# Where the 64x64 triangular inverses of a chunked recurrence are made: GpSimd with 32x32 blocks, or GpSimd with 16x16 blocks and TensorE

## The chip, the cores and the metric

The kernel runs on one core of one Trainium2 chip. The metric is device time in microseconds, the median of the runs; lower is better.

## What is computed

The program is three transformer layers in a row on a sequence of 512 positions with 1024 channels, all in float32 (large matmuls as three products of split float32r halves). The change touches the mixer of the third layer, an RWKV-7 recurrence over 16 heads of 64 channels, once forward and once backward in time:

```
def rwkv7_scan(r, w, k, v, kk, a):
    def step(state, inp):
        r_t, w_t, k_t, v_t, kk_t, a_t = inp
        sa = jnp.einsum('bhvk,bhk->bhv', state, -kk_t)
        state = (state * w_t[:, :, None, :] + sa[..., None] * (kk_t * a_t)[:, :, None, :]
                 + v_t[..., None] * k_t[:, :, None, :])
        return state, jnp.einsum('bhvk,bhk->bhv', state, r_t)
...
    for d in range(2):
        w_log = -jax.nn.softplus(-(w0[d] + jnp.tanh(xw @ w1[d]) @ w2[d])) - 0.5
        decay = jnp.exp(-jnp.exp(w_log.astype(F32)))
        a = jax.nn.sigmoid(a0[d] + (xa @ a1[d]) @ a2[d])
...
        o = rwkv7_scan(*ins)
...
        dir_out.append((group_norm(o, gn_w, gn_b) + bonus.reshape(nB, S, D)) * g.astype(F32))
    y = dir_out[0] + dir_out[1]
    return y.astype(h.dtype) @ w_o
```

The kernel does not step through 512 positions. It cuts them into 8 chunks of 64 and, in each chunk and head, solves with a unit triangular 64x64 matrix I + L. The inverse of that matrix is what the change is about.

## The kernel before

The recurrence is the function `rwkv`. Two heads fill the 128 partitions (head h on partitions 64h to 64h+63), so there are 8 head pairs; with two directions that makes 16 rounds, `q = 0..15`, `p, d = divmod(q, 2)`. A round has four stages, each a Python generator whose `yield`s cut it into steps:

- `pair` (once per two rounds) loads k and r of a head pair and its small weights, and makes normalised keys.
- `prep` makes decays and scaled operands (`ar`, `bk`), multiplies them into `sc` (L1310 on TensorE, masked out of PSUM by VectorE in L1313), and makes the other operands `vs`, `tb`, `za`, `kb`. `sc` holds the triangular matrices; its diagonal 32x32 blocks go to DRAM as `lu` (L1320, queue SP). There are 2 heads x 2 blocks x 8 chunks = 32 such blocks.
- `invert` reads them back as `lt` (L1371), one block per partition and four copies of the 32 blocks, each copy for a quarter of the columns. GpSimd then does 31 elimination steps of two instructions: a product `tmp` (L1378) and a subtraction from `x` (L1380). The result goes to DRAM as `xu` (L1387) and back into the 64x64 layout as `X` (L1391). VectorE transposes the first block (L1399), TensorE multiplies twice (L1406, L1415) and VectorE writes the off-diagonal block (L1419). That completes the inverse.
- `scan` uses `X` (L1434) and then runs the chain over the chunks: six pairs of a TensorE product (L1468) and a VectorE update of `n` (L1469), output products (L1463, L1473) and group norm, gate and accumulation (L1478 to L1504).

Two fillers of lower priority run beside them: `values` (v projection, L1204) and `output` (output projection, L1217, added up by VectorE in L1219). Both load weights through queue SP (L1199, L1211).

A loop over a step counter `t` starts `prep`, `invert` and `scan` of a round at steps 0, 9 and 36 of that round, a round begins every 16 steps, and every step advances each live generator by one `yield`. This gives the order in which instructions are written; a scheduler then orders each engine by priority and by when a buffer slot of a pool is free, and every engine and DMA queue executes its list strictly in order. Pool `bk` has two slots; pool `un` (`lt`, `x`, `tmp`) has one; PSUM pool `psm` has four; `wr`, for the fillers' weights, has three.

Below, a round's "period" is the distance from one round's transposition L1399 to the next one's.

Of the kernel before, what the change touches and what calls it, by code (L numbers as in the profile page):

```python
# [8 lines left out]
F32 = mybir.dt.float32  # L9
F32R = mybir.dt.float32r  # L10
AF = mybir.ActivationFunctionType
# [5 lines left out]
HP, HPA, HPB, HPS, HPO, HP1, HP1B = 300, 50, 50, -300, 0, 300, 300  # L17
S = 512
D = 1024
NT = D // 128  # L20
# [989 lines left out]
class L3:  # L1010
# [117 lines left out]
    def rwkv(self, lp, rkd, vm, tw, ta, sg):  # L1128
        nc, tc, I = self.nc, self.tc, self.I
        with ExitStack() as cx:  # L1130
            pool = lambda n, b, **kw: cx.enter_context(tc.tile_pool(name=n, bufs=b, **kw))
            arp, vsp, bkp, unp, sp, wk = (pool(n, b) for n, b in (
                ("ar", 4), ("vs", 3), ("bk", 2), ("un", 1), ("s3", 2), ("wk", 2)))
            scp = pool("psc", 1, space=PSUM)
            fil = pool("psf", 2, space=PSUM)
            pop = pool("pso3", 1, space=PSUM)
# [1 line left out]
            nc.sync.dma_start(K3, I["const3"])  # L1138
            mask, cmask, cmat, bones = K3[:, 0:128], K3[:, 128:640], K3[:, 640:768], K3[:, 768:770]
            bfull = K3[:, 770:898]  # L1140
            xeye = lp.tile([128, 8, 32], F32, name="xeye")
            nc.sync.dma_start(xeye, I["xeye"])
            gneps = lp.tile([128, 1], F32, name="gneps")
            nc.vector.memset(gneps, 64e-5)
# [4 lines left out]
            a = VEC_AT["k_a"]  # L1149
# [29 lines left out]
            def T():  # L1179
                turn[0] += 1  # L1180
                p, tag = ((sp, "t3"), (self.tmp, "t"), (self.tmp, "t"))[turn[0] % 3]
                return p.tile([128, S], F32, tag=tag, name=tag)
# [82 lines left out]
            def prep(q, C):  # L1265

                p, d = divmod(q, 2)
# [22 lines left out]
                ar = C["ar"] = arp.tile([128, 2, S], F32, tag="ar", name="ar", bufs=3)  # L1290
                ar0, ar1 = ar[:, 0], ar[:, 1]

                bk = bkp.tile([128, 8, 2, 64], F32, tag="bk", name="bk")
# [10 lines left out]
                sc = C["sc"] = [w4(h).rearrange("p (c t) -> p c t", c=8) for h in range(2)]  # L1304
                for g in range(2):
# [7 lines left out]
                        nc.vector.tensor_tensor(sc[h][:, 4 * g:4 * g + 4, :], ps[h].rearrange("p c a t -> p c (a t)"),  # L1313
                                                mask.unsqueeze(1).to_broadcast([128, 4, 128]), op=ALU.mult)
                    yield
                lu = C["lu"] = self.dram.tile([32, 32, 32], F32, tag="lu", name="lu", bufs=2)
                for h in range(2):
                    for b in range(2):
                        p0, u0 = 64 * h + 32 * b, (h * 2 + b) * 8
                        nc.sync.dma_start(lu[u0:u0 + 8].rearrange("c s t -> s c t"),  # L1320
                                          sc[h][p0:p0 + 32, :, 32 * b:32 * b + 32])

                nc.vector.tensor_tensor(kd, flip(r[p], d), kd, op=ALU.mult)
                if d:
# [4 lines left out]
                vs = C["vs"] = vsp.tile([128, 8, 2, 64], F32, tag="vs", name="vs")  # L1329
# [36 lines left out]
            def invert(q, C):  # L1366


                lt = unp.tile([128, 32, 32], F32, tag="lt", name="lt")
                for f in range(4):  # L1370
                    nc.sync.dma_start(lt[32 * f:32 * f + 32], C["lu"])  # L1371
                x = unp.tile([128, 8, 32], F32, tag="x", name="x")
                nc.gpsimd.tensor_copy(x, xeye)
                yield
                for i in range(31):
                    m, n = i // 4 + 1, 31 - i
                    t = unp.tile([128, 80], F32, tag="tmp", name="tmp")[:, :m * n].rearrange("p (m n) -> p m n", m=m)
                    nc.gpsimd.tensor_tensor(t, x[:, :m, i:i + 1].to_broadcast([128, m, n]),  # L1378
                                            lt[:, i:i + 1, i + 1:].to_broadcast([128, m, n]), op=ALU.mult)
                    nc.gpsimd.tensor_tensor(x[:, :m, i + 1:], x[:, :m, i + 1:], t, op=ALU.subtract)  # L1380
                    if i % 2 == 2 - 1:
                        yield
                X = C["x"] = self.hp.tile([128, 8, 64], F32, tag="h", name="X")
                nc.gpsimd.memset(X, 0.0)
                xu = self.dram.tile([32, 8, 4, 32], F32, tag="xu", name="xu", bufs=2)
                for f in range(4):
                    nc.sync.dma_start(xu[:, :, f, :], x[32 * f:32 * f + 32])  # L1387
                for h in range(2):
                    for b in range(2):
                        p0, u0 = 64 * h + 32 * b, (h * 2 + b) * 8  # L1390
                        nc.sync.dma_start(X[p0:p0 + 32, :, 32 * b:32 * b + 32],  # L1391
                                          xu[u0:u0 + 8].rearrange("c m f t -> (m f) c t"))
                yield
                for _ in range(5):
                    yield

                sc = C["sc"]
                t1 = T()[:, :256].rearrange("p (c t) -> p c t", c=8)
                nc.vector.transpose(t1, X[:, :, 0:32])  # L1399
                yield  # L1400
                qt = T()[:, :256].rearrange("p (c t) -> p c t", c=8)
                pq = self.psm.tile([128, 2, 8, 32], F32, tag="mm", name="mm")
                for c in range(8):
                    for h in range(2):
                        a = 64 * h
                        nc.tensor.matmul(pq[a + 32:a + 64, 0, c, :], sc[h][a:a + 32, c, 32:64], t1[a:a + 32, c, :],  # L1406
                                         start=True, stop=True, tile_position=(a, a + 32))
                for h in range(2):
                    a = 64 * h
                    nc.scalar.activation(qt[a + 32:a + 64], pq[a + 32:a + 64, 0], AF.Copy, scale=-1.0)  # L1410
                yield
                for c in range(8):
                    for h in range(2):
                        a = 64 * h
                        nc.tensor.matmul(pq[a:a + 32, 1, c, :], qt[a + 32:a + 64, c, :], X[a + 32:a + 64, c, 32:64],  # L1415
                                         start=True, stop=True, tile_position=(a + 32, a))
                for h in range(2):
                    a = 64 * h
                    nc.vector.tensor_copy(X[a:a + 32, :, 32:64], pq[a:a + 32, 1])  # L1419
                yield  # L1420

            def scan(q, C):
# [78 lines left out]
                else:  # L1501
# [6 lines left out]
            Cs = [{} for _ in range(NQ)]  # L1508
            stages = [lambda q: prep(q, Cs[q]), lambda q: invert(q, Cs[q]), lambda q: scan(q, Cs[q]), lambda q: pair(q // 2)]
            fills = sorted([(2 * 16 * (p - 1) + 2, self.ahead(values(p), HPS)) for p in range(1, NT)] +  # L1510
                           [(2 * 16 * p + 78, self.ahead(output(p), HPS)) for p in range(NT)], key=lambda x: x[0])
            for _ in values(0):
                pass
            live, lf = [], []
            t = -4
            while t <= 36 + (NQ - 1) * 16 or live or lf or fills:
                for st, at in ((2, 36), (1, 9), (0, 0), (3, -4)):
                    q, e = divmod(t - at, 16)
                    if e == 0 and 0 <= q < NQ and not (st == 3 and q % 2):
                        live.append((st, q, stages[st](q)))  # L1520
                live.sort(key=lambda x: (-x[0] % 4, x[1]))
                live = [x for x in live if next(x[2], 0) != 0]
                while fills and fills[0][0] <= t:
                    lf.append(fills.pop(0)[1])
                if t % 3 == 0:
                    lf = [x for x in lf if next(x, 0) != 0]
                t += 1
# [112 lines left out]
def constants():  # L1640

    import numpy as np
    f = np.float32
    i, t = np.arange(128), np.arange(64)
    a = {"upper": (i[:, None] <= i[None]).astype(f)}
    a["causal"] = np.concatenate([np.zeros((128, 384), f), np.where(i[None] <= i[:, None], 0, -1e30).astype(f)], 1)
    n = np.arange(32)
    cm = np.zeros((128, 4, 33), f)
    for b in range(4):
        ok = (16 * n[None] + 31 <= (b * 128 + i)[:, None]) & (n[None] < 31)  # L1650
        cm[:, b, :32] = np.where(ok, 0, -1e30)
        cm[:, b, 32] = ok.any(1)
    a["cmp_mask"] = cm

    d = np.arange(1024) - 512
    n = np.abs(d)
    large = np.minimum(8 + (np.log(np.maximum(n, 1).astype(f) / f(8)) / f(math.log(128)) * f(8)).astype(np.int32), 15)
    bucket = np.where(d > 0, 16, 0) + np.where(n < 8, n, large)
    a["onehot"] = (bucket[None] == np.arange(32)[:, None]).astype(f)
    c = (n <= 64) * 1 + ((n % 4 == 0) & (n <= 256)) * 1 + (n % 16 == 0) * 1  # L1660
    lnc = np.zeros((16, 1024), f)
    lnc[:8] = np.where(c > 0, np.log(np.maximum(c, 1)), -1e30)
    lnc[8:] = np.where(n <= 128, 0, -1e30)
    a["lnc"] = lnc

    s = i % 64
    mask = np.concatenate([s[:, None] < t[None], s[:, None] <= t[None]], 1)
    starts = np.broadcast_to(np.arange(S) % 64 != 0, (128, S))
    same = i[:, None] // 64 == i[None] // 64
    a["const3"] = np.concatenate([mask, starts, np.eye(128) - same / 64, i[:, None] // 64 == np.arange(2)[None], same], 1).astype(f)  # L1670
    x = np.zeros((4, 32, 8, 32), f)
    for h in range(4):
        for m in range(8):
            x[h, :, m, 4 * m + h] = 1
    a["xeye"] = x.reshape(128, 8, 32)
    return a


# [14 lines left out]
```

## Time and profile before

| quantity | value |
|---|---|
| median of 3 runs | 3077.1 us (3075.54 to 3078.77) |
| time of the profiled execution | 3076.38 us |
| its span, first to last instruction | 3074.6 us |
| share of the span busy: PE, DVE, ACT, POOL | 93%, 54%, 44%, 13% |
| L1378 and L1380 on POOL, busy | 165.0 and 168.5 us, 496 instructions each |
| mean granted TensorE clock | 0.959 |

The engines are named as the profile does: PE is TensorE, DVE VectorE, ACT ScalarE, POOL GpSimd, SP the queue that issues most DMAs. The recurrence occupies the span from about 2000 to 2670 us; outside it POOL is nearly idle. A float32 matmul leaves two records in the trace for one instruction of the program.

### The profile page before, as it was taken

What the parts mean: (1) busy time and instruction counts of PE and PEld (TensorE: products, weight loads), DVE (VectorE), ACT (ScalarE), POOL (GpSimd) and SP (SyncE); (2) the same over time, 40 slices, a digit from 0 to 9 for tenths busy, and PEclk for the clock granted to TensorE, in tenths of its full rate; (3) what the DMA queues carried; (4) which work ended last, traced back from release to release, by engine and by line L of the source; (5) the groups of instructions that cost most, each with busy time, mean ns of one, the idle gap of its engine ahead of it and who ended that gap; (6) DMA issues with size and microseconds to landing.
All of it is one profiled execution on the core that took longest, in us unless ns stands there. A gap on an engine that the chain in (4) does not pass through costs nothing.

```text
span 3074.6 us, 49553 instructions
## 1 busy us (share of the span) xinstructions
PE 2859.1 (93%) x19720; PEld 2302.1 (75%) x19720; DVE 1671.7 (54%) x3427; ACT 1356.4 (44%) x2460; POOL 386.7 (13%) x1116
## 2 busy tenths in 40 slices
PE   7999999999999999899999999977788888599998
PEld 6877778778898889776988888856555556388887
DVE  5566684554462335766733446945555656553445
ACT  5565652663342223555532333744454443243222
POOL 0000000000000000000000000025555555100000
PEclk9999999999999999999999999986888989799999
DMA  4311122224223323221233233321111212213331
GB/s 138 96 38 49 42 90 90 93 77 139 93 74 105 96 92 95 79 83 41 88 96 95 92 108 109 105 63 42 36 43 50 56 41 56 86 63 96 92 107 42
DMA packets 139415, 243.99 MB, mean 79 GB/s; under 512 B 62064, under 2 KB 82288, under 8 KB 139056
## 3 DMA queue, kind: packets, MB, share of 16 engines
q1 hardware_dynamic: 136864, 238.90, 25.4%
q8 instruction: 155, 2.54, 0.3%
q10 hardware_dynamic: 2320, 1.93, 0.2%
q14 instruction: 76, 0.62, 0.1%
HBM read 228.13 MB, written 12.65 MB: 78 GB/s over the span
## 4 chain that ended last, share of the span: by engine, by line
PE 74%; POOL 9%; DVE 6%; issue 4%; DMA 3%; ACT 2%; SPq 2%; POOLq 0%; ACTq 0%; DVEq 0%
PE mm L80 57%; POOL x L1380 4%; POOL tmp L1378 4%; PE o L732 1%; PE mm L416 1%; PE mm L1090 1%; PE tr L722 1%; PE o L950 1%; PE fil L1204 1%; DMA lt<-lu 1%; PE mm L761 1%; PE tr L924 1%; DVE sqa L265 1%; PE mm L903 1%; SPq L1391 1%
## 5 line engine op out<-in xcount | busy, mean ns | idle before, releaser
L80 PE MATMUL mm<-xh,wh 128*128 128x512 f32 (+1 forms) x2072 | 739.1, 358 | 10.4 <-ACT xh L69 6.3
L80 PE MATMUL mm<-xl,wh 128*128 128x512 f32 (+1 forms) x2072 | 735.9, 356 | 0.3 <-DVE xl L70 0.3
L80 PE MATMUL mm<-xh,wl 128*128 128x512 f32 (+1 forms) x2072 | 732.4, 355 | 2.3 <-DVE wl L65 2.3
L63 ACT CAST wh<-wr 128x1024 fp32r<-128x1024 f32 (+1 forms) x343 | 357.0, 1044 | 757.7 <-PE mm L80 616.2
L65 DVE TENSOR_TENSOR wl<-wr,wh 128x1024 fp32r<-128x1024 f32 (+1 forms) x343 | 416.6, 1217 | 457.1 <-ACT wh L63 447.2
L80 PEld LDWEIGHTS mm<-xh,wh 128*128 128x128 f32 x2072 | 392.0, 190 | 73.3 <-ACT xh L69 7.4
L80 PEld LDWEIGHTS mm<-xh,wl 128*128 128x128 f32 x2072 | 391.7, 189 | 61.0 <-issue 3.5
L80 PEld LDWEIGHTS mm<-xl,wh 128*128 128x128 f32 x2072 | 391.7, 189 | 56.6 <-issue 3.3
L80 PE MATMUL mm<-hl,wh 128*128 128x512 f32 (+1 forms) x880 | 304.9, 347 | 0.0
L80 PE MATMUL mm<-hh,wh 128*128 128x512 f32 (+1 forms) x880 | 303.7, 346 | 0.0
L80 PE MATMUL mm<-hh,wl 128*128 128x512 f32 (+1 forms) x880 | 303.5, 345 | 0.0
L275 POOL TENSOR_TENSOR r<-r,mhalf 128x2 f32<-128x2 f32 x24 | 25.9, 1080 | 1284.4 <-DVE r L274 1284.4
L1378 POOL TENSOR_TENSOR tmp<-x,lt 128x60 f32<-128x60 f32 (+24 forms) x496 | 165.0, 333 | 167.2 <-DMA lt<-lu 120.1
L80 PEld LDWEIGHTS mm<-hl,wh 128*128 128x128 f32 x880 | 166.4, 189 | 22.4 <-DVE hl L70 0.5
L80 PEld LDWEIGHTS mm<-hh,wl 128*128 128x128 f32 x880 | 166.2, 189 | 21.9
L80 PEld LDWEIGHTS mm<-hh,wh 128*128 128x128 f32 x880 | 166.2, 189 | 21.8
L1380 POOL TENSOR_TENSOR x<-x,tmp 128x60 f32<-128x60 f32 (+24 forms) x496 | 168.5, 340 | 38.8
L241 DVE TENSOR_TENSOR acc<-acc,mm 128x256 f32<-128x256 f32 (+1 forms) x88 | 47.4, 541 | 178.3 <-PE mm L80 178.3
L265 DVE TENSOR_TENSOR sqa<-sqa,sq 128x256 f32<-128x256 f32 x182 | 75.3, 422 | 57.3 <-ACT sq L264 53.3
L69 ACT CAST hh<-t 128x512 fp32r<-128x512 f32 (+1 forms) x106 | 57.0, 539 | 77.6 <-DVE t L212 68.5
L674 DVE CUSTOM_DVE_ANT_0 s<-mm,cmask 128x128 f32<-128x128 f32 (+3 forms) x128 | 59.9, 487 | 46.9 <-PE mm L756 23.1
L70 DVE TENSOR_TENSOR hl<-t,hh 128x512 fp32r<-128x512 f32 (+1 forms) x106 | 62.2, 589 | 35.3 <-ACT hh L69 34.6
(398 smaller groups left out, 4842.0 us busy)
## 6 DMA issues: line engine op xcount, KB each, us to landing
wr<-in_mlp_w_dram SPq DMA_DIRECT2D x128, 512.0 KB, 3.6
wr<-in_w_ffn_in_dram SPq DMA_DIRECT2D x44, 512.0 KB, 3.6
wr<-in_w_mg_dram SPq DMA_DIRECT2D x24, 512.0 KB, 3.7
wr<-in_w_br_dram SPq DMA_DIRECT2D x24, 512.0 KB, 3.6
wr<-in_attn_w_in_dram SPq DMA_DIRECT2D x18, 512.0 KB, 3.6
wr<-in_w_ffn_out_dram SPq DMA_DIRECT2D x16, 512.0 KB, 3.5
lt<-lu SPq DMA_DIRECT2D x64, 128.0 KB, 2.6
wr<-in_w_kv_dram SPq DMA_DIRECT2D x12, 512.0 KB, 3.9
```

The costliest lines, as they stand in the source:

```text
L63: nc.scalar.copy(hi, raw)
L65: nc.vector.tensor_tensor(lo, raw, hi.bitcast(F32), op=ALU.subtract)
L69: self.nc.scalar.copy(hi, src)
L70: self.nc.vector.tensor_tensor(lo, src, hi.bitcast(F32), op=ALU.subtract)
L80: nc.tensor.matmul(ps, l, r[:, s0:s1], start=(n == 0), stop=(n == 3 * nk - 1))
L241: nc.vector.tensor_tensor(a, a, ps, op=ALU.add)
L265: nc.vector.tensor_tensor(self.acc, self.acc, t, op=ALU.add)
L416: nc.tensor.matmul(ps[:, b % 2, :], l[:, t], r, start=(n == 0), stop=(n == 23))
L674: nc.vector.tensor_tensor_reduce(s, ps, mask, -1.0, 3e38, ADD, ALU.min, m)
L722: nc.tensor.transpose(ps[:, b, :], s[:, b * 128:(b + 1) * 128], self.ident)
L1378: nc.gpsimd.tensor_tensor(t, x[:, :m, i:i + 1].to_broadcast([128, m, n]), lt[:, i:i + 1, i + 1:].to_broadcast([128, m, n]), op=ALU.mult)
L1380: nc.gpsimd.tensor_tensor(x[:, :m, i + 1:], x[:, :m, i + 1:], t, op=ALU.subtract)
```

## The change

GpSimd inverts 64 blocks of 16x16 instead of 32 blocks of 32x32: 15 elimination steps instead of 31, on two copies instead of four. A new piece in `invert` then joins pairs of 16x16 inverses into 32x32 inverses: a VectorE transposition of all of `X` (L1399 of the changed kernel), 32 TensorE products 32x32 by 16 columns (L1406), a negating ScalarE copy (L1408), 32 products 16x16 by 16 (L1412), and four copies into `X` (L1415, two on ScalarE, two on VectorE). The rest of `invert` follows as before, with lines 20 higher (L1419, L1426, L1430, L1435, L1439); `scan` too (L1454 is the former L1434, L1488 the former L1468, L1489 the former L1469). DMAs through `lu` and `X` become eight instead of four, those of `lt` and `xu` two instead of four. Pool `un` gets two slots and `bk` one. `scan` starts at step 31, and the output fillers five steps sooner.

```
-                ("ar", 4), ("vs", 3), ("bk", 2), ("un", 1), ("s3", 2), ("wk", 2)))
+                ("ar", 4), ("vs", 3), ("bk", 1), ("un", 2), ("s3", 2), ("wk", 2)))
...
-                lu = C["lu"] = self.dram.tile([32, 32, 32], F32, tag="lu", name="lu", bufs=2)
+                lu = C["lu"] = self.dram.tile([64, 16, 16], F32, tag="lu", name="lu", bufs=2)
                 for h in range(2):
-                    for b in range(2):
-                        p0, u0 = 64 * h + 32 * b, (h * 2 + b) * 8
+                    for b in range(4):
+                        p0, u0 = 64 * h + 16 * b, (h * 4 + b) * 8
                         nc.sync.dma_start(lu[u0:u0 + 8].rearrange("c s t -> s c t"),
-                                          sc[h][p0:p0 + 32, :, 32 * b:32 * b + 32])
+                                          sc[h][p0:p0 + 16, :, 16 * b:16 * b + 16])
...
-                lt = unp.tile([128, 32, 32], F32, tag="lt", name="lt")
-                for f in range(4):
-                    nc.sync.dma_start(lt[32 * f:32 * f + 32], C["lu"])
+                lt = unp.tile([128, 16, 16], F32, tag="lt", name="lt")
+                for f in range(2):
+                    nc.sync.dma_start(lt[64 * f:64 * f + 64], C["lu"])
...
-                for i in range(31):
-                    m, n = i // 4 + 1, 31 - i
+                for i in range(15):
+                    m, n = i // 2 + 1, 15 - i
...
-                for f in range(4):
-                    nc.sync.dma_start(xu[:, :, f, :], x[32 * f:32 * f + 32])
+                for f in range(2):
+                    nc.sync.dma_start(xu[:, :, f, :], x[64 * f:64 * f + 64])
                 for h in range(2):
-                    for b in range(2):
...
+                    for b in range(4):
...
                 sc = C["sc"]
+                xt = T().rearrange("p (c t) -> p c t", c=8)
+                nc.vector.transpose(xt, X)
+                yield
+                Q = [(h, b, 64 * h + 32 * b, 32 * b) for h in range(2) for b in range(2)]
+                q16 = T()[:, :128].rearrange("p (c t) -> p c t", c=8)
+                pq = self.psm.tile([128, 2, 8, 16], F32, tag="mm", name="mm")
+                for c in range(8):
+                    for h, b, a, o in Q:
+                        nc.tensor.matmul(pq[a:a + 32, 0, c, :], sc[h][a:a + 32, c, o:o + 32], xt[a:a + 32, c, o:o + 16],
+                                         start=True, stop=True, tile_position=(a, a))
+                nc.scalar.activation(q16, pq[:, 0], AF.Copy, scale=-1.0)
+                yield
+                for c in range(8):
+                    for h, b, a, o in Q:
+                        nc.tensor.matmul(pq[a:a + 16, 1, c, :], q16[a:a + 32, c, :], X[a:a + 32, c, o + 16:o + 32],
+                                         start=True, stop=True, tile_position=(a, a))
+                for h, b, a, o in Q:
+                    (nc.vector.tensor_copy if b else nc.scalar.copy)(X[a:a + 16, :, o + 16:o + 32], pq[a:a + 16, 1])
+                yield
...
-                           [(2 * 16 * p + 78, self.ahead(output(p), HPS)) for p in range(NT)], key=lambda x: x[0])
+                           [(2 * 16 * p + 73, self.ahead(output(p), HPS)) for p in range(NT)], key=lambda x: x[0])
...
-                for st, at in ((2, 36), (1, 9), (0, 0), (3, -4)):
+                for st, at in ((2, 31), (1, 9), (0, 0), (3, -4)):
```

How the lists of the engines change is shown at three places in the middle of the recurrence.

Queue SP, one round, before (`w_o` is a filler's weight):

```order
L1387 DMA xu<-x 256x1x32 x4
L1320 DMA lu<-wh 32x8x32 x2
L1320 DMA lu<-wl 32x8x32 x2
L1391 DMA X<-xu 32x8x32 x4
L1371 DMA lt<-lu 32x1024 x4
L1211 DMA wr<-in_rk_w_o_dram 128x8x128
```

Queue SP, one round, after (`w_20217` is the small weight of the gate):

```order
L1320 DMA lu<-wh 16x8x16 x4
L1320 DMA lu<-wl 16x8x16 x4
L1371 DMA lt<-lu 64x256 x2
L1387 DMA xu<-x 512x1x16 x2
L1238 DMA w_20217<-in_rk_lora_dram 128x128
L1391 DMA X<-xu 16x8x16 x8
```

Before, the next round's `lu` stood between a round's `xu` and its `X`; now all four transfers of one round stand together, and the next round's `lu` comes behind this round's `X`.

VectorE where it takes up `X`, before (L1469 is the chain over the chunks):

```order
L1469 SCALAR_TENSOR_TENSOR n<-sc_21932,dl,n 128x64 x2
L1166 RECIPROCAL hs<-hs 128x8
L1170 COPY t<-hs 128x512
L1399 STREAM_TRANSPOSE t<-X 128x256
L1469 SCALAR_TENSOR_TENSOR n<-sc_21932,dl,n 128x64
L1219 TENSOR_TENSOR y<-y,fil 128x512
L1259 TENSOR_TENSOR kk<-t,mm 128x512
```

VectorE at the same place, after:

```order
L1489 SCALAR_TENSOR_TENSOR n<-sc_21607,dl,n 128x64
L1323 TENSOR_TENSOR t<-r,t 128x512
L1489 SCALAR_TENSOR_TENSOR n<-sc_21607,dl,n 128x64
L1399 STREAM_TRANSPOSE t_21718<-X 128x512
L1281 MEMSET dp 128x8
L1313 TENSOR_TENSOR wh<-mm,const_17834 128x512
L1313 TENSOR_TENSOR wl<-mm,const_17834 128x512
L1489 SCALAR_TENSOR_TENSOR n<-sc_21607,dl,n 128x64
L1219 TENSOR_TENSOR y<-y,fil 128x512
L1313 TENSOR_TENSOR wh<-mm,const_17834 128x512
L1313 TENSOR_TENSOR wl<-mm,const_17834 128x512
L1489 SCALAR_TENSOR_TENSOR n<-sc_21607,dl,n 128x64
```

The transposition moved from behind five of the six chain updates to between the third and the fourth, and right ahead of the L1313 that make `sc` of the next round; before, those came more than twenty rows later.

TensorE at the joining of the blocks, before (`fil` is filler work):

```order
L1406 MATMUL mm<-t,wl 32x32
L1217 MATMUL fil<-ys,wr 128x512
L1204 MATMUL fil<-vm,wr 128x512
L1217 MATMUL fil<-ys,wr 128x512 x3
L1415 MATMUL mm<-X,t 32x32 x16
L1491 MATMUL mm<-ident,t 64x64 x16
```

TensorE at the joining of the blocks, after (L1426 is the former L1406):

```order
L1406 MATMUL mm<-t_21718,wl 32x16 x2
L1361 MATMUL mm<-ident,bk 128x64 x16
L1412 MATMUL mm<-X,t 16x16 x32
L1217 MATMUL fil<-ys,wr 128x512 x2
L1426 MATMUL mm<-t_21887,wh 32x32
L1426 MATMUL mm<-t_21887,wl 32x32
```

The new products stand ahead of the old ones with the next round's transposes (L1361) and a few fillers between them.

## Rows read from the trace of the kernel before

**Rows 1.** By stretch: length; busy PE, PEld, DVE, ACT, POOL; PEclk; DMA share; GB/s.

```profile
2114.71:2151.22 36.51, 28.81 (x448) 24.06 (x450) 19.21 (x38) 16.64 (x32) 20.84 (x65) 0.73 0.16 39
2339.82:2376.05 36.23, 27.34 (x415) 20.30 (x414) 18.38 (x40) 13.23 (x24) 21.22 (x64) 0.88 0.19 47
2376.05:2415.22 39.17, 37.25 (x480) 23.56 (x479) 25.40 (x47) 19.62 (x34) 22.72 (x65) 0.89 0.20 47
2114.71:2565.80 451.09, 379.42 (x5318) 267.80 (x5318) 256.59 (x500) 208.95 (x368) 262.75 (x768) 0.87 0.19 45
```

**Rows 2.** Waits of PE, 2080 to 2606 us: waiter, releaser: total, times, longest.

```profile
PE mm L1406 <- DVE t L1399: 42.5, 7, 8.9
PE o L1473 <- DVE n L1469: 31.6, 5, 8.5
```

**Rows 3.** Waits of DVE and of POOL in the same stretch.

```profile
DVE t L1399 <- DMA X<-xu: 79.7, 13, 9.3
...
POOL tmp L1378 <- DMA lt<-lu: 81.1, 13, 7.6
```

**Rows 4.** Timeline of POOL around the end of one inversion.

```profile
2287.49 0.20 POOL L1378 TENSOR_TENSOR tmp<-x,lt 128x8 f32<-128x8 f32 x1
2287.78 0.21 POOL L1380 TENSOR_TENSOR x<-x,tmp 128x8 f32<-128x8 f32 x1
...
2300.05 0.24 POOL L1378 TENSOR_TENSOR tmp<-x,lt 128x31 f32<-128x31 f32 x1 [7.17 <-DMA lt<-lu]
```

**Rows 5.** Timeline of queue SP in the same gap (time to issue).

```profile
2288.01 2.52 SPq L1387 DMA_DIRECT2D xu<-x  x4
2290.63 1.04 SPq L1320 DMA_DIRECT2D lu<-wh  x2
...
2292.91 1.78 SPq L1391 DMA_DIRECT2D X<-xu  x4
2294.86 1.72 SPq L1371 DMA_DIRECT2D lt<-lu  x4
```

**Rows 6.** Pieces of the chain that ended last: landing of the four transfers.

```profile
2290.63 1.73 DMA lu<-wh
...
2517.09 1.97 DMA xu<-x
...
2521.24 1.85 DMA X<-xu
...
2563.03 2.65 DMA lt<-lu
```

**Rows 7.** First POOL product, and first and last (sixteenth) L1399 on DVE.

```profile
2043.96 0.79 POOL L1378 TENSOR_TENSOR tmp<-x,lt 128x31 f32<-128x31 f32 x1 [38.97 <-DMA lt<-lu]
...
2077.50 0.45 DVE L1399 STREAM_TRANSPOSE t<-X 128x256 f32<-128x256 f32 x1 [10.91 <-DMA X<-xu]
...
2632.74 0.45 DVE L1399 STREAM_TRANSPOSE t<-X 128x256 f32<-128x256 f32 x1 [8.48 <-DMA X<-xu]
```

**Rows 8.** Groups on DVE, 2114.71 to 2565.8 us: busy us, mean ns.

```profile
L1469 DVE SCALAR_TENSOR_TENSOR n<-sc,dl,n 128x64 f32<-128x64 f32 x72 | 20.3, 282 | 57.0 <-PE sc L1468 44.2 <-PE mm L1352 12.7
L1313 DVE TENSOR_TENSOR wh<-mm,const 128x512 f32<-128x512 f32 x24 | 16.4, 684 | 6.5 <-PE mm L1310 6.3
```

**Rows 9.** Small products: a timeline piece of PE, a group 2112 to 2119 us.

```profile
2310.38 0.69 PE L1415 MATMUL mm<-X,t 32*32 32x32 f32 x32
...
L1415 PE MATMUL mm<-X,t 32*32 32x32 f32 x32 | 1.1, 236 | 0.9 <-issue 0.9
```

**Rows 10.** Timelines of DVE and ACT: the copies of the block products.

```profile
2311.78 0.86 DVE L1419 COPY X<-mm 32x256 f32<-32x256 f32 x2
...
2338.96 0.76 ACT L1410 ACTIVATE t<-mm 32x256 f32<-32x256 f32 x2
```

**Rows 11.** Groups on PE, 2114.71 to 2565.8 us: the fillers.

```profile
L1217 PE MATMUL fil<-ys,wr 128*128 128x512 f32 x82 | 53.5, 741 | 5.1 <-DVE y L1219 4.0 <-ACT y L1221 1.2
L1204 PE MATMUL fil<-vm,wr 128*128 128x512 f32 x64 | 39.4, 726 | 0.0
```

More of the change, by code (lines that the diff above doesn't have):

```diff
@@ L1140, in rwkv @@
             bfull = K3[:, 770:898]
-            xeye = lp.tile([128, 8, 32], F32, name="xeye")
+            xeye = lp.tile([128, 8, 16], F32, name="xeye")
             nc.sync.dma_start(xeye, I["xeye"])
@@ L1366, in invert @@
             def invert(q, C):
-                lt = unp.tile([128, 32, 32], F32, tag="lt", name="lt")
-                for f in range(4):
-                    nc.sync.dma_start(lt[32 * f:32 * f + 32], C["lu"])
-                x = unp.tile([128, 8, 32], F32, tag="x", name="x")
+                lt = unp.tile([128, 16, 16], F32, tag="lt", name="lt")
+                for f in range(2):
+                    nc.sync.dma_start(lt[64 * f:64 * f + 64], C["lu"])
+                x = unp.tile([128, 8, 16], F32, tag="x", name="x")
                 nc.gpsimd.tensor_copy(x, xeye)
                 yield
-                for i in range(31):
-                    m, n = i // 4 + 1, 31 - i
-                    t = unp.tile([128, 80], F32, tag="tmp", name="tmp")[:, :m * n].rearrange("p (m n) -> p m n", m=m)
+                for i in range(15):
+                    m, n = i // 2 + 1, 15 - i
+                    t = unp.tile([128, 40], F32, tag="tmp", name="tmp")[:, :m * n].rearrange("p (m n) -> p m n", m=m)
                     nc.gpsimd.tensor_tensor(t, x[:, :m, i:i + 1].to_broadcast([128, m, n]),
@@ L1380, in invert @@
                     nc.gpsimd.tensor_tensor(x[:, :m, i + 1:], x[:, :m, i + 1:], t, op=ALU.subtract)
-                    if i % 2 == 2 - 1:
+                    if i % 2:
                         yield
@@ L1384, in invert @@
                 nc.gpsimd.memset(X, 0.0)
-                xu = self.dram.tile([32, 8, 4, 32], F32, tag="xu", name="xu", bufs=2)
-                for f in range(4):
-                    nc.sync.dma_start(xu[:, :, f, :], x[32 * f:32 * f + 32])
+                xu = self.dram.tile([64, 8, 2, 16], F32, tag="xu", name="xu", bufs=2)
+                for f in range(2):
+                    nc.sync.dma_start(xu[:, :, f, :], x[64 * f:64 * f + 64])
                 for h in range(2):
-                    for b in range(2):
-                        p0, u0 = 64 * h + 32 * b, (h * 2 + b) * 8
-                        nc.sync.dma_start(X[p0:p0 + 32, :, 32 * b:32 * b + 32],
+                    for b in range(4):
+                        p0, u0 = 64 * h + 16 * b, (h * 4 + b) * 8
+                        nc.sync.dma_start(X[p0:p0 + 16, :, 16 * b:16 * b + 16],
                                           xu[u0:u0 + 8].rearrange("c m f t -> (m f) c t"))
@@ L1670, in constants @@
     a["const3"] = np.concatenate([mask, starts, np.eye(128) - same / 64, i[:, None] // 64 == np.arange(2)[None], same], 1).astype(f)
-    x = np.zeros((4, 32, 8, 32), f)
-    for h in range(4):
+    x = np.zeros((2, 64, 8, 16), f)
+    for h in range(2):
         for m in range(8):
-            x[h, :, m, 4 * m + h] = 1
-    a["xeye"] = x.reshape(128, 8, 32)
+            x[h, :, m, 2 * m + h] = 1
+    a["xeye"] = x.reshape(128, 8, 16)
     return a
```

## The prediction

> **What bounds the kernel now.** Only the third layer's recurrence changes, so I read only its stretch. The busy times by stretch come first: over twelve periods PE is busy 379.42 of 451.09 us, which is 31.6 of 37.6 us a period; POOL is busy 262.75 us, 21.9 a period, and DVE and ACT less than 60% [rows 1]. No engine is full. The waits tell why. PE's two long ones are behind L1399 (42.5 us) and behind the chain update L1469 (31.6 us) [rows 2], and on DVE one wait stands out: L1399 itself for the transfer `X<-xu`, 79.7 us in 13 rounds [rows 3]. The wait for L1469 is the same wait seen later, because L1399 stands among the chain updates and DVE works in order. Together that is 74 us of PE idle in about 14 periods, 5 to 6 us each, nearly all the idle time PE has (71.7 us in twelve periods). POOL in turn waits 81.1 us for `lt<-lu` [rows 3].
>
> So a ring closes through POOL: elimination, `xu` out, `X` in, the next `lt` in, elimination. The timelines show one turn. POOL ends at 2287.99 and starts the next elimination at 2300.05, 12.1 us later [rows 4]; in that gap SP issues `xu`, `lu`, `X` and `lt` one behind the other for 8.6 us, and then `lt` lands [rows 5, 6]. Elimination itself is the rest of the period, about 25.5 us. The distance of the first and last L1399 gives the period: (2632.74 - 2077.50)/15 = 37.0 us [rows 7].
>
> **The change part by part.**
>
> *Elimination on POOL.* 62 instructions become 30, of 8 to 36 elements a partition. One of 31 elements takes 0.24 us, one of 8 elements 0.20, and the next starts 0.09 after its end [rows 4]; 30 at 0.32 from start to start are 9.6 us. A whole run takes longer than its undisturbed rows would, so I take 10.5 us. About 15 us leave POOL's part.
>
> *The ring afterwards.* The lists show that the second slot of `lt` and `x` will hold nothing of use: on SP a round's `lu`, `lt`, `xu` and `X` stand together, and on DVE L1399 of a round stands right ahead of the L1313 that make the next round's `sc`. So one set of coefficients is in flight at a time and a new ring closes through DVE, SP and POOL. Its turn: L1399, now 512 wide, 0.9 us (twice 0.45 [rows 7]); four L1313 of 0.68 and one chain update of 0.28 [rows 8], overlapping a little, 2.8; eight `lu` at 0.5 each [rows 5], of which the first half starts under the last L1313, 3.5, and landing 1.73 [rows 6]; two `lt`, 0.9, landing 2.65; elimination 10.5; two `xu` at 0.63 and 0.2 to start, 1.5, landing 1.97; eight `X` at 0.45, 3.7, landing 1.85; between them some 0.3. The sum is 32.3 us. Bounds: 31 with a run of 9.6 us and faster landing of the smaller `lt`; 35 with the old share of slow POOL instructions and a filler's addition (L1219) among the L1313, as the list has it. The `lu`, `xu` and `X` pieces are half as long (64 bytes instead of 128) and as many in all; I take the old landing times.
>
> *New work on PE.* 64 instructions a round, 128 records. The nearest are those of L1415: 32 records in 0.69 us when PE had been running, 1.1 us just after a wait [rows 9], so 21 to 34 ns each. With half the columns and four blocks side by side instead of two I take 16 ns, 2.1 us a round; bounds 1.4 and 4.4.
>
> The Trainium skill speaks against this piece: "TensorEngine Tiling (Array Packing)", section Instruction Overhead, says that each matmul carries about 60 cycles, so that one with a free dimension of 1 takes as long as one with 60. By it 128 records would cost 3.2 us at 2.4 GHz, 1.1 more than I take. L1415's records, 32 columns wide, follow each other in less than that (21 ns against 25 ns) [rows 9].
>
> *New waits on PE.* The joining is a series: L1406, ACT L1408, L1412, four copies, a transposition, and only then the old two products with their copies. Between L1412 and L1426 PE has to wait for copies and transposition, about 0.4 + 0.45 + hand-overs, and longer where ACT has L1363 ahead, some 1.3 to 2.3 us; between L1426 and L1435 for 0.76 us of copying and hand-overs, about 0.9; the old copies behind L1435 are 0.86 us [rows 10]. And since `scan` now starts sooner, DVE makes the next round's operands (L1294 to L1301, seven instructions, most of a size like L1313's 0.68 us [rows 8]) between the first chain updates, during which PE has only the chain. These holes sum to about 8 us a period, an estimate from these rows. The fillers, (53.5 + 39.4)/12 = 7.7 us a period [rows 11], were put into just them, and they no longer run in the wait for `X`, which is gone. I take 1.1 us a period as uncovered; bounds 0 and 2.9. If the fillers' cover is gone (in the first and last rounds there are none), PE has time anyway: such rounds have 27 to 29 us of PE work [rows 1].
>
> *The period.* PE: 31.6 + 2.1 + 1.1 = 34.8 us, above the ring's 32.3. Rounds with few fillers will be nearer the ring (27.34 + 2.1 + holes), rounds with many above the mean (37.25 busy in one [rows 1]). I take 34.7.
>
> *Ends.* In the first round nothing hides elimination: from POOL's start to L1399 it is 33.5 us [rows 7]. Now it is 10.5 to 12 for elimination, 9 for `xu` and `X`, and `lu` takes 1.5 longer before it: 12 us saved. After the last L1399 the joining is added: half a microsecond of transposition, 2.1 to 4.4 of products, copies: 4 us lost.
>
> *Costed at nothing.* `bk` with one slot: the next round's L1296 comes half a period after PE's last reading of it (L1361); if that cover were gone, DVE would wait for the 16 transposes of L1361, about 1 us by the records of L1415 [rows 9]. The output fillers' start moves with `scan`. SP's other loads (L1238, L1251, L1252) stand between `xu` and `X` and lie under the landing of `xu`; L1199 and L1211 stand under elimination or ahead of `lu`; without cover each is one issue, 0.4 to 0.5 us, unless it waits for a buffer.
>
> *The sum.* 12 + 15 x (37.0 - 34.7) - 4 = 42.5 us off the profiled execution's 3076.38, which lies 0.7 below the median of 3077.1 and 1.8 above its span: **3034 us**.
>
> **The rivals.**
>
> *The ring alone sets the pace.* If fillers cover all holes and running PE steadily keeps its clock up (0.87 on average [rows 1]; nearer 1.0 its 31.6 us shrink), the period is 32.3: 12 + 15 x 4.7 - 4 = 78 us, 2998 us. For it: nearly all PE idle is one wait [rows 2], which vanishes. Against: 31.6 us of PE work is not made less by it, except through the clock.
>
> *PE is fuller than I think.* The new products at the bound of 4.4 us with no more holes, or the holes uncovered with the products as taken, make a period of about 36.3: 12 + 15 x 0.7 - 4 = 18 us, 3058 us. For it: after-wait rows cost 34 ns a record [rows 9], and periods with many fillers are full of PE work already, 37.25 of 39.17 us [rows 1]. By the Trainium skill's 60 cycles alone, see above, the period would be 35.8 and the time 3050 us.
>
> *Slower: the wait leaves DVE and comes back on PE.* The joining adds five hand-overs between PE, ACT and DVE in a row, to a list in which `prep`, chain and joining now alternate. The gain is used up when the period reaches 37.0 + 8/15 = 37.55, that is when new products and uncovered holes together cost 5.9 us a period where I take 3.2. With both bounds, 4.4 and 2.9, the period is 38.9 and the time 3076 + 15 x 1.9 - 8 = 3097 us. For it: holes of 8 us are there, and fillers are unevenly spread. Against: both bounds at once are needed in all rounds.
>
> *No change that can be told.* 37.4 to 38 us a period by the same sums, or the ring held up where SP waits for a filler's buffer (L1211 stands between `lt` and `xu`): 10 us beyond elimination in half of the rounds would do it.
>
> **How the numbers follow.** Forecast (34 to 35.6, 3020 to 3045): 0.47. Ring (down to 32.3, 2998 to 3020): 0.20. Fuller PE (35.6 to 37.1, 3045 to 3070): 0.20. No change: 0.04. Slower: 0.09. About 0.2% (6 us) is what a measurement of this kernel can tell from no change. Faster by more than that holds all of the first three, 0.87; same 0.04; slower 0.09. The range must reach into both neighbours: 2998, the ring's own time, to 3068, near the end of the fuller PE; it leaves about 0.04 below and 0.13 above.
>
> **What will show it.** Right, if L1399's wait for `X` falls from 5 to 6 us a round to 2 or less; POOL's runs take 10 to 11 us and POOL idles two thirds of the period; the distance between L1399 is 34 to 35.5 us; the first L1399 comes near 2066 us. L1406 and L1412 should take about 1 us each. Wrong on the side of the ring, if DVE's wait for `X` stays 3 us or more a round while PE waits behind it at a period near 32 to 33; wrong on the slow side, if PE waits for L1415, L1419 or the chain update instead, a total over 5 us a round. The second slot of `lt` is shown useless if `lt` of a round never lands before POOL has ended the round before.

## The result and the profile after

The changed kernel takes 3046.6 us (3044.85 to 3048.25), the kernel before 3077.9 beside it; the ratio is 0.9899, 95% interval 0.9881 to 0.9916. It is faster by 31 us, 13 us short of the 44 forecast; 3046.6 lies inside the range and just over the upper end of the likeliest case.

The page of the changed kernel begins with its span and each engine's busy time:

```profile
span 3046.5 us, 53309 instructions
...
PE 2872.4 (94%) x21768; PEld 2330.7 (77%) x21768; DVE 1685.9 (55%) x3475; ACT 1337.1 (44%) x2489; POOL 168.1 (6%) x604
```

Span less PE busy is PE's idle time: 174.1 us, where the kernel before had 3074.6 - 2859.1 = 215.5. So 41.4 us of idle time went and 13.3 us of work came: 28.1 less.

First the transposition that the forecast followed (its first and last start, then what held it):

```profile
L1399 DVE STREAM_TRANSPOSE t<-X x16: 700/712/712, 2066.6 to 2595.9; 128x512 f32<-128x512 f32 x16
its engine sat idle before it (us, times) until:
  DMA X<-xu: 12.9, 2
```

The wait for `X`, before 99.1 us in 15 of the 16 rounds (79.7 in 13 in the stretch of [rows 3]), is 12.9 us in two, 11.1 of it in the first round, which nothing precedes. GpSimd, in the timeline of one run (start, duration, engine, line):

```profile
2111.80 0.22 POOL L1378 TENSOR_TENSOR tmp<-x,lt 128x15 f32<-128x15 f32 x1 [25.47 <-DMA lt<-lu]
...
2120.89 0.21 POOL L1380 TENSOR_TENSOR x<-x,tmp 128x8 f32<-128x8 f32 x1
```

A run takes 9.3 us and stands behind a wait of 25 us for `lt`; as the wait for `X` is gone, GpSimd has left the path, and e4_slow2 below tells by how much. Now the stretch between the first and the last L1399, 15 periods, of the kernel before and of the changed one (length, then busy time of PE, PEld, DVE, ACT, POOL, granted clock):

```profile
2077.50:2632.74 555.24, 455.16 (x6448) 322.96 (x6448) 311.35 (x607) 243.84 (x433) 324.42 (x959) 0.86 0.18 45
```

```profile
2066.62:2595.94 529.32, 461.97 (x8377) 347.29 (x8378) 322.64 (x650) 232.66 (x469) 120.05 (x478) 0.88 0.14 31
```

A period went from 37.02 us (PE busy 30.34, idle 6.67) to 35.29 (busy 30.80, idle 4.49). Most of the 4.49 stands in the five largest waits of PE in the changed kernel from 2063 to 2560 us (total, times, longest):

```profile
PE mm L1310 <- DVE ar L1301: 17.0, 5, 4.4
PE mm L1426 <- DVE t L1419: 10.8, 8, 3.4
PE sc L1488 <- DVE n L1489: 9.0, 10, 2.6
PE mm L1406 <- DVE t L1399: 8.5, 1, 8.5
PE mm L1310 <- DVE bk L1300: 7.6, 5, 3.0
```

L1310, the next pass's scores, waited 0.4 us for `ar` in this stretch of the kernel before; it now waits 24.6 us for `ar` and `bk`. One such place, on DVE and then on PE:

```profile
2272.69 0.28 DVE L1489 SCALAR_TENSOR_TENSOR n<-sc,dl,n 128x64 f32<-128x64 f32 x1
...
2272.96 0.69 DVE L1294 TENSOR_TENSOR ar<-kk,dp 128x512 f32<-128x512 f32 x1
...
2274.16 1.39 DVE L1296 TENSOR_TENSOR bk<-t,t 64x512 f32<-64x512 f32 x2
2275.56 1.39 DVE L1300 TENSOR_TENSOR bk<-t,t 64x512 f32<-64x512 f32 x2
2276.98 0.69 DVE L1301 TENSOR_TENSOR ar<-r,dp 128x512 f32<-128x512 f32 x1
2277.59 0.28 DVE L1489 SCALAR_TENSOR_TENSOR n<-sc,dl,n 128x64 f32<-128x64 f32 x1
```

```profile
2273.03 0.33 PE L1488 MATMUL sc<-n,m 64*64 64x64 f32 x4
2273.19 0.40 PE L1493 MATMUL o<-n,ar 64*64 64x64 f32 x6
2273.52 1.13 PE L1217 MATMUL fil<-ys,wr 128*128 128x512 f32 x2
2277.81 0.80 PE L1310 MATMUL mm<-ar,bk 64*128 64x128 f32 x4 [3.17 <-DVE ar L1301]
```

Between two chain updates stand 4.7 us of DVE work on the next pass's operands. PE has a filler for 1.1 us of it and then idles 3.17.

### The profile page after: what moved, and what is told of

Read it like the earlier page. It is cut to its first block, busy times and chain, and to the rows that moved or that the text cites. A ratio compares the mean times of both kernels' runs of the same rounds, so it can differ in the third digit from the quotient of the medians.

```text
span 3046.5 us, 53309 instructions
## 1 busy us (share of the span) xinstructions
PE 2872.4 (94%) x21768; PEld 2330.7 (77%) x21768; DVE 1685.9 (55%) x3475; ACT 1337.1 (44%) x2489; POOL 168.1 (6%) x604
## 4 chain that ended last, share of the span: by engine, by line
PE 81%; DVE 9%; ACT 5%; issue 2%; DMA 1%; POOL 1%; SPq 1%; DVEq 0%; POOLq 0%; ACTq 0%
PE mm L80 58%; PE mm L1090 2%; PE fil L1204 2%; PE o L732 2%; PE mm L416 1%; PE mm L1310 1%; PE tr L722 1%; PE o L950 1%; PE mm L761 1%; PE mm L1454 1%; PE tr L924 1%; DVE sqa L265 1%; PE mm L903 1%; PE mm L1245 1%; PE mm L1511 1%
## 5 line engine op out<-in xcount | busy, mean ns | idle before, releaser
L1337 ACT COPY vs<-mm 64x256 f32<-64x256 f32 x64 | 23.4, 366 | 165.6 <-PE mm L1332 164.7
L1310 PE MATMUL mm<-ar,bk 64*128 64x128 f32 x512 | 61.9, 369 | 29.0 <-DVE ar L1301 17.0
L1310 PEld LDWEIGHTS mm<-ar,bk 64*128 64x128 f32 x512 | 51.6, 258 | 40.3 <-issue 36.5
```

The costliest lines, as they stand in the source:

```text
L1310: nc.tensor.matmul(ps[h][:, c], bk[rw, cc].rearrange("p a t -> p (a t)"), ar[rw, :, cc * 64:(cc + 1) * 64], start=True, stop=True)
```

## The experiments

All ratios are against runs of the kernel before on the same chip. Theory, throughout: the shorter elimination takes GpSimd out of the ring, and joining and new holes on PE give part of it back. What is asked is which part of the change gives what.

**The start of the recurrence.** Three kernels move it.

```
e1_late:  after,  ((2, 31) -> ((2, 36);  2 * 16 * p + 73 -> + 78
e5_b31:   before, ((2, 36) -> ((2, 31);  + 78 -> + 73;  without "for _ in range(5): yield" ahead of t1
e9_fil78: after,  + 73 -> + 78 alone
```

> The changed kernel with scan back at step 36 and the output fillers back by five steps; nothing else. Theory (the shorter elimination took the wait for X away, and PE's own list now sets a period of about 35): 3036 to 3056 us, near the changed kernel's 3046.6, since PE's work is the same and only the holes lie elsewhere. Rival (the sooner recurrence is what gives): at least half of the 31 us are lost, 3062 us or more.

> The kernel before with the recurrence five steps sooner (scan at step 31, five empty steps of invert taken out, output fillers five steps sooner), GpSimd still with 31 steps on 32x32 blocks and one slot. Theory (elimination of 25 us in the ring sets the period): no gain, 3068 to 3095 us. Rival (the sooner recurrence gives): 3062 us or less.

> The changed kernel with the output fillers back at 78 and the recurrence left at 31. Theory (of the two lines that were moved by five steps it is the recurrence that costs time, since its chain stands among the next pass's preparation; the fillers only fill): no change, 3040 to 3052. Rival (the fillers, which come five steps sooner, are what costs): most of the 21 us, 3024 to 3033.

Measured: e1_late 3025.4 us (0.9831, 0.9811 to 0.9851), e5_b31 3104.9 (1.0086, 1.0071 to 1.0101), e9_fil78 3046.0 (0.9890, 0.9874 to 0.9906). Both theories on the sooner start were wrong, and both rivals as well, which lay on the other side: starting sooner costs 21 us in the new kernel and 27 us in the old one (there the empty steps ahead of the transposition went too). The fillers' start costs nothing, as expected. The waits of PE in e1_late, the same stretch:

```profile
PE fil L1217 <- DVE y L1219: 9.9, 7, 2.1
PE mm L1406 <- DVE t L1399: 8.5, 1, 8.5
PE mm L1511 <- DVE t L1506: 7.7, 2, 4.9
PE mm L1310 <- DVE wh L1313: 5.8, 3, 4.6
...
PE mm L1426 <- DVE t L1419: 3.1, 4, 1.9
...
PE mm L1310 <- DVE ar L1301: 1.2, 1, 1.2
PE sc L1488 <- DVE n L1489: 0.6, 3, 0.3
```

and in e5_b31, which has neither joining nor short elimination (L1403 is the former L1406, its chain's lines are L1465 and L1466):

```profile
PE mm L1403 <- DVE rs L1479: 35.7, 6, 6.7
PE mm L1403 <- DVE t L1396: 32.6, 5, 19.5
PE mm L1310 <- DVE ar L1301: 16.3, 5, 4.4
```

The wait for `ar` comes and goes with the start at 31: 0.4 us before, 16.3 in e5_b31; 17.0 after, 1.2 in e1_late. It is not the only wait that moves. In e1_late those of L1310 for `ar` and `bk`, of L1426 and of L1488 are 39.5 us shorter, others are longer or new (L1217, L1511, L1310 for `wh`), and PE's idle time falls by 18.5 us in the 15 periods. In e5_b31 the wait for `X` stays (78.9 us in 13 rounds), and with it PE's long waits, now in L1403. With the start at 36 the six chain updates stand in steps 7 to 12 of the round of 16, behind the preparation; with 31 in steps 2 to 7, among it. The same stretch, L1399 to L1399, of e1_late:

```profile
2062.20:2563.20 501.00, 452.17 (x8342) 334.39 (x8342) 321.43 (x642) 246.55 (x476) 132.42 (x477) 0.91 0.15 33
```

A period is 33.4 us, idle 3.26 and busy 30.14 instead of 4.49 and 30.80: two thirds of the gain is idle time, one third is PE's work, which took less time at a granted clock of 0.91 instead of 0.88. The split is that of two executions: the profiled one of e1_late was its fastest (3020.5 us), that of the changed kernel its slowest (3048.3), so they lie 28 us apart and the medians 21.

**The buffers.**

```
e2_un1:  after,  ("un", 2) -> ("un", 1)
e6_bun2: before, ("bk", 2), ("un", 1) -> ("bk", 1), ("un", 2)
```

> The changed kernel with one slot for lt, x and tmp instead of two. The lists of PE, DVE, ACT and SP are the same as in the changed kernel, so only waits can differ. Theory (one set of coefficients is in flight at a time, so the second slot holds nothing): 3046.6 within 4 us. Rival (the slot hides the load of the next set): 0.3 to 3 us a period are lost, 3051 to 3090 us.

> The kernel before with two slots for lt, x and tmp and one for bk; the lists of PE, DVE, ACT and SP are the same as in the kernel before. Theory (SP issues the next lt behind X in its own order, so a free slot does not bring it sooner): 3070 to 3081 us, no change. Rival (the wait for the slot is part of the 12 us between eliminations): 1 to 5 us a period, 3000 to 3062 us.

Measured: e2_un1 3045.6 us (0.9893, 0.9873 to 0.9914), e6_bun2 3079.0 (1.0004, 0.9994 to 1.0013). Neither does anything: the second slot gains nothing, and one slot of `bk` costs nothing at the old start. At 31 no run has two slots of `bk`; the waits of DVE in the changed kernel list none for it.

**The price of the joining.** One kernel leaves it out, one issues its products twice.

```
e7_nojoin: after without the lines from "xt = T()" to the copies of L1415; three empty yields for them
e8_join2:  after, "for _ in range(2):" around each matmul of L1406 and of L1412
```

> The changed kernel without the lines that join the 16x16 inverses (transpose L1399, products L1406 and L1412, their copies; three empty steps stand in their place, and the off-diagonal 16x16 blocks of the 32x32 inverses stay zero, so this part of the result is left out). Theory (the join costs its products on TensorE, 1.4 us a round as in the profile of the changed kernel, and the waits of L1406 and L1426 on VectorE, 8.5 + 14.2 us in all, go with it): 15 x 1.4 + some 15 to 20 = 36 to 41 us less, so 3003 to 3015. Rival (the join lies in time that is idle anyway, because the rounds wait elsewhere): 3030 or more.

> The changed kernel with each product of L1406 and of L1412 issued twice (same result). Theory (a narrow product costs TensorE 11 ns, and TensorE sets the rounds): 15 x 1.4 = 21 us more at full clock, so 3060 to 3070. Rival A (the products fall into idle time): 3042 to 3052. Rival B (a narrow product costs the 60 cycles of the page's rule, 25 to 50 ns, of which the records show only a part): 3.2 to 6.4 us a round, 3095 or more.

Measured: e7_nojoin 3002.9 us (0.9756, 0.9741 to 0.9770), e8_join2 3091.7 (1.0045, 1.0030 to 1.0060). The joining costs 44 us in all, slightly above the theory. e8_join2 came out 45 us slower, twice the theory's 21 and just short of rival B. All products L1406 and L1412 of the changed kernel, by shape (busy us, mean ns of one):

```profile
L1406 PE MATMUL mm<-t,wl 32*32 32x16 f32 x512 | 11.7, 182 | 0.0
L1406 PE MATMUL mm<-t,wh 32*32 32x16 f32 x512 | 11.4, 181 | 8.5 <-DVE t L1399 8.5
...
L1412 PE MATMUL mm<-X,t 32*16 32x16 f32 x1024 | 11.3, 175 | 0.6 <-issue 0.6
```

The two halves of L1406 lie over each other; together they are busy for 11.95 us, which with 11.3 is 23.3 for 2048 records, 11 ns each. In e8_join2 the same two lines, doubled, in 15 of the 16 rounds (the line's busy time on PE and PEld, then the clock); its stretch from the first to the last L1399; and two of its waits:

```profile
2060.00:2640.00 580.00, 23.58 (x1920) 21.46 (x1920) 0.84 0.13 29
...
2060.00:2640.00 580.00, 22.19 (x1920) 19.32 (x1920) 0.84 0.13 29
```

```profile
2060.60:2638.10 577.50, 502.18 (x10298) 375.18 (x10298) 322.28 (x651) 234.78 (x469) 117.36 (x478) 0.84 0.13 29
```

```profile
PE mm L1414 <- issue: 10.2, 13, 1.5
...
PE mm L1407 <- issue: 5.6, 7, 1.2
```

The products take 45.8 us for 3840 records, 12 ns each, so as rows they doubled and no more: 45.8/15 - 23.3/16 = 1.6 us a period. The period rose by 3.21, from 35.29 to 38.50: PE busy from 30.80 to 33.48, idle from 4.49 to 5.02. So 1.1 us of the 3.21 is the other work of the period, which takes longer while the granted clock is 0.84 instead of 0.88, and 0.5 is idle time. The profile puts 15.8 us of idle time ahead of these products down to issue, that is, to nothing that it shows; elsewhere PE waits less. In the end 2048 added records whose rows say 11 ns cost 45.1 us, 22 ns each; why the granted clock fell is not shown.

e7_nojoin divides its 44 us in another way: without the joining PE is busy 27.0 us less (2845.4), 13 ns for each of the 2048 records, and idle 17.4 us less (3002.1 - 2845.4 = 156.7): the waits of L1406 and L1426, 8.5 and 10.8 us in the changed kernel, go, and smaller ones change. The next pass's scores still wait, from 2063 to 2560 us:

```profile
PE mm L1310 <- DVE ar L1301: 17.1, 5, 4.4
...
PE mm L1310 <- DVE bk L1300: 6.2, 4, 1.9
```

So these holes come with the sooner start and not with the joining.

**The ring's reserve.**

```
e4_slow2: after, "for _ in range(2):" around the product of L1378
```

> The changed kernel with each product of L1378 on GpSimd issued twice, which lengthens a GpSimd run from 9.3 to some 14 us and leaves everything else. Theory (the ring of scores, DMA, GpSimd, DMA and chain has some 0 to 1.5 us to spare in the short rounds and 5 to 7 in the long ones, which a pair of rounds can share): 9.4 us more in a pair of rounds against 6 to 8 to spare, 8 to 25 us more, so 3055 to 3072. Rival A (the ring has nothing to spare and binds): 15 x 4.7 = 70 more, 3110 or more. Rival B (it has 5 us and more to spare in every round): 3042 to 3052.

Measured: 3089.8 us (1.0040, 1.0025 to 1.0055), between theory and rival A. A GpSimd run now takes 14.0 us, 4.7 more, and the transposition (L1400 here) waits for `X` again:

```profile
L1400 DVE STREAM_TRANSPOSE t<-X x16: 704/711/712, 2069.5 to 2641.5; 128x512 f32<-128x512 f32 x16
its engine sat idle before it (us, times) until:
  DMA X<-xu: 53.5, 8
```

```profile
PE sc L1489 <- DVE n L1490: 39.7, 14, 9.8
```

The period is (2641.5 - 2069.5)/15 = 38.13 us, 2.84 longer for 4.7 us of elimination. The ring had 1.9 us a round to spare, where I had read 3 to 4 from a pair of rounds; it closes at about 35.3 - 1.9 = 33.4 us, an estimate from these two kernels that holds if the ring sets the pace of e4_slow2 throughout. The wait for `X` shows there in the first round (13.5 us) and in seven of the other fifteen (40.1). The long wait of the chain L1489 is the wait for `X` seen later, as in the kernel before.

**Versions with the recurrence later.**

```
e10_at34:            after, recurrence at 34, fillers at 76
e11_36_gap8:         e1_late,  eight empty yields ahead of L1399 instead of five
e12_34_gap8:         e10_at34, eight instead of five
e13_36_gap8_pools:   e11_36_gap8 with ("bk", 2), ("un", 1)
```

> The changed kernel with the recurrence started at step 34 and the output fillers at 76, between the changed kernel's 31 and 73 and the 36 and 78 of the kernel before. Theory (what counts is where in the round of 16 steps the six chain updates of L1488 and L1489 stand: at 31 they fall into steps 2 to 7, in which the next pass's preparation needs VectorE, at 36 into steps 7 to 12, behind it; at 34 into 5 to 10, most of them behind it): most of the gain of 36, 3020 to 3034. Rival (every step sooner costs the same, 21 us over 5 steps): 3046 - 3 x 4.2 = 3034 with a spread to 3031 to 3037; a third (each step sooner gains, and 36 was a chance): 3037 or more.

> The changed kernel with the recurrence at 36, the fillers at 78 (as in e1_late, 3025.4) and eight empty steps instead of five ahead of L1399, so that VectorE comes to the transpose three steps later. Theory (in e1_late VectorE still stands in L1399 for 22.1 us in five rounds, 10.8 of them in the first, until X lands, and what is queued behind it waits; three steps later X is there): up to 11 us less than e1_late, 3012 to 3022. Rival (these waits lie in time that TensorE fills anyway, or the joining products now meet the chain of the recurrence and make new waits): 3023 or more.

> The changed kernel with the recurrence at 34, the fillers at 76 (as in e10_at34, 3034.0) and eight empty steps ahead of L1399. Theory (in e10_at34 VectorE stands in L1399 for 32.9 us in eight rounds until X lands, and the chain updates L1489 queued behind it make TensorE wait 21.5 us in nine; with the transpose three steps later these go): 10 to 22 us less, 3012 to 3024. Rival (the place of the chain at 34 costs, not the wait for X): 3028 or more.

> As e11_36_gap8, with the buffers as in the kernel before: two slots of bk, one of un. Theory (neither buffer is waited for: the profile of e11_36_gap8 lists no wait on L1300 and GpSimd has 10 us of work in a round of 31): the same as e11_36_gap8, 3012 to 3023. Rival A (with one slot of bk VectorE comes late to the next pass's bk, which TensorE then misses in L1310): 3010 or less. Rival B (the second slot of un is what lets GpSimd start soon enough at this shorter round): 3025 or more.

Measured: e10_at34 3034.0 us (0.9850, 0.9833 to 0.9867), which fits the theory's edge and its rival and decides nothing; e11_36_gap8 3017.8 (0.9801, 0.9781 to 0.9821); e12_34_gap8 3021.6 (0.9814, 0.9799 to 0.9829); e13_36_gap8_pools 3019.3 (0.9818, 0.9797 to 0.9839), no different from e11_36_gap8, as expected. e11_36_gap8 is the fastest whole kernel found, 2.0% ahead of the kernel before and 1% of the changed one; that it beats e1_late is not certain, since the intervals overlap.

Three more empty steps did not take the wait of L1399 away. In e11_36_gap8 it is

```profile
  DMA X<-xu: 15.1, 5
  DMA lu<-wh: 10.6, 1
```

The first round, which nothing precedes, has a wait of about 11 us in each of these kernels; the profile puts it down to `lu` here and to `X` in e1_late (10.8 of its 22.1 us). Outside it the wait is 11.3 us in four rounds in e1_late and 15.1 in five here, so the theory's range was met, but not for its reason. With the recurrence at 34, first e10_at34's part for the first round, then e12_34_gap8:

```profile
  DMA lu<-wh: 11.0, 1
```

```profile
  DMA X<-xu: 41.1, 9
```

```profile
2064.16 0.71 DVE L1399 STREAM_TRANSPOSE t<-X 128x512 f32<-128x512 f32 x1 [10.88 <-DMA X<-xu]
```

Outside the first round that is 32.9 us in e10_at34 and 30.2 in e12_34_gap8, each in eight rounds, and the wait of the chain product L1488, which should have gone, grew from 18.9 to 37.6 us (2063 to 2560 us). PE's idle time is 162.1 us (3017.4 - 2855.3) against 160.5 in e10_at34. What fell is PE's busy time, by 16 us. From the first to the last L1399, e10_at34 and then e12_34_gap8:

```profile
2064.70:2583.10 518.40, 464.19 (x8358) 342.88 (x8358) 317.65 (x645) 239.62 (x471) 139.32 (x477) 0.87 0.14 31
```

```profile
2064.20:2567.40 503.20, 447.68 (x8339) 335.32 (x8340) 318.03 (x645) 232.17 (x466) 142.36 (x477) 0.89 0.15 32
```

PE's work took 1.1 us a period less, at a granted clock of 0.89 instead of 0.87; by the ratio of the clocks 0.7 us would be expected, an estimate from these rows. Why the clock was higher with no less idle time stays open.

## Why the forecast was right, and where it was off

| term | forecast | measured |
|---|---|---|
| first L1399 sooner | 12 | 10.9 (2077.50 to 2066.62) |
| period | 37.0 to 34.7 | 37.02 to 35.29 |
| lost after the last L1399 | 4 | 8.7 (441.9 to 450.6 us to the span's end) |
| sum, 15 periods | 42.5 | 10.9 + 26.0 - 8.7 = 28.1 |

- *The wait for `X` vanishes, the second slot holds nothing, `bk` costs nothing*: right, by the wait of L1399 and by e2_un1 and e6_bun2 (for `bk` at the old start only).
- *Elimination 10.5 us*: 9.3. *The ring, 32.3 with bounds 31 and 35*: about 33.4 by e4_slow2, behind PE as forecast. The wait of 5 to 6 us a round fell to 0.1 outside the first round.
- *The period*: that 34.7 came within 0.6 us of 35.29 is in good part luck, since two errors nearly cancel. PE's work was put at 31.6 + 2.1 = 33.7 us and measured 30.80, 2.9 less; its idle time was put at 1.1 and measured 4.49, 3.4 more. Of the 2.9, 1.3 come from a mixture: 31.6 is PE's work in the twelve middle periods, of 37.6 us, and the fifteen to which the sum applies it had 30.34 of 37.02. 0.65 come from the products, and 1.0 from other work that took less time while the granted clock was 0.88 instead of 0.86.
- *New products 2.1 us, bounds 1.4 and 4.4*: their records are busy 1.45 us a period, near the lower bound. Doubling them cost 3.0 us a round, in part through clock and idle time; leaving the joining out gained 44/15 = 2.9 us a round, ends included, of which 1.2 are idle time. The Trainium skill, "TensorEngine Tiling (Array Packing)", section Instruction Overhead, gives some 60 cycles to each matmul. At 2.4 GHz that is 25 ns, an estimate from the page's figure. The prediction counted it for each record, and 11 ns lie below it. Counted for each instruction, which leaves two records, it would be 12.5 ns a record and 1.6 us a round, near the 1.45; the 22 ns of a doubled record are then 44 ns an instruction. Which of the two is meant, no run here shows.
- *Holes of 8 us, of which fillers leave 1.1 uncovered, bounds 0 and 2.9*: this step failed, and beyond its bound, which had been given without a working. 4.49 us a period were idle. The place was named rightly, the next pass's operands between the first chain updates; that the fillers "were put into just them" was wrong. At the place shown one pair of filler products covered 1.1 us of the 4.7 us on DVE. e1_late and e5_b31 show that these holes come with the sooner recurrence, e7_nojoin that they stay without the joining. They are not all of the 4.49: with the start at 36 there are still 3.26, and leaving the joining out took 17.4 us of idle time from the whole, 1.2 a period.
- *After the last L1399, 4 us*: 8.7, and not as waits. From there to the end of the span, before and after:

```profile
2632.74:3074.60 441.86, 399.06 (x2330) 339.60 (x2330) 209.93 (x371) 144.32 (x248) 7.44 (x6) 0.94 0.27 84
```

```profile
2595.94:3046.50 450.56, 407.74 (x2488) 345.02 (x2486) 216.36 (x384) 146.10 (x253) 7.45 (x6) 0.93 0.25 82
```

  PE is idle for 42.8 us in both; what came is 8.7 us of work. Of the 158 records more, 128 are the last round's joining, 1.45 us a round; the rest is work that now stands behind L1399, which has moved ahead of more of the chain updates. From L1399 to the first of the old products it was 0.6 us before (2632.74 to 2633.33) and is 8.0 now (2595.94 to 2603.95), and PE is busy for 6.9 of them. So the term measures where the mark stands more than what the joining costs.
- *PE is fuller than I think, 3045 to 3070*: 3046.6 lies at the edge of this rival. Of its two conditions the uncovered holes came, and went beyond their bound; the expensive products did not show in their rows.
- *Slower, by holes and products of 5.9 us together*: did not come, yet the sooner start made the old kernel slower (e5_b31), so the holes are real and were paid from the gain. *The ring alone, 2998 us*: e7_nojoin shows what stood between, 3002.9 without the joining.

In parts: short elimination with joining gives 52 us at the old start (e1_late), the sooner start takes 21 back, the buffers and the fillers' start do nothing that can be told.

## What to carry to other kernels

When a stage gets shorter, moving its consumer up by the time saved is a change of its own: here it put a chain with one short update per step into the steps in which the same in-order engine makes the next round's operands, and cost 40% of what the shorter stage had won. Price a hole by what the engine's own list holds right behind it, not by the sum of filler work in the round. And price a series of narrow products by leaving it out and by doubling it, since neither shows in its rows alone: here leaving it out took idle time away too, 17 of 44 us, and doubling it cost 45 us where the rows grew by 24.

## What the runs showed of the hardware

- 64 records of 32x16 follow each other in 0.69 us, 11 ns each, in the same time as 32 records of 32x32 took before [rows 9]. Issued twice as often they take 12 ns, but PE is idle for 15.8 us that the profile puts down to issue (0.6 in the changed kernel, 3.6 in e1_late), and the other work of a period takes 1.1 us longer at a mean granted clock of 0.84 instead of 0.88, between the levels of 1.2 and 2.4 GHz. One such series in the changed kernel:

```profile
2600.25 0.69 PE L1412 MATMUL mm<-X,t 32*16 32x16 f32 x64
```

- The mean granted clock over the recurrence was 0.86 with 6.67 us of idle time a period, 0.88 with 4.49 and 0.91 with 3.26 (e1_late), where the period fell by 1.89 us for 1.23 of idle time. Idle time alone does not set it: e8_join2 had 0.84 with 5.02, e10_at34 0.87 with 3.61, and e12_34_gap8 0.89 with 3.70. What else does is not shown.
- The transposition of 128x512 took 0.71 us, not twice the 0.45 of 128x256.
